# Weight sums by on-chip accumulating transfers, and the DVE order at the start of the feed-forward layer

## The chip, the cores and the metric

The kernel runs on one core of one Trainium2 chip. The metric is device time in microseconds of one launch. The kernel before the change took 1691.21 us (median of three runs, 1689.07 to 1691.75).

## The reference

Two layers work on `x` of 512 tokens by 1024 channels, all in float32. What matters here is the second half of the mixer and the feed-forward part:

```
for l in range(DEPTH):                       # DEPTH = 2
    h = rmsnorm(x, norm1_g[l])
    x = x + gated_parallel_mixer(h, ...)     # ends in: merged @ w_out, w_out 1024 x 1024
    h = rmsnorm(x, norm2_g[l])
    x = x + conv_ffn(h, w_up[l], conv_w[l], conv_b[l], w_down[l])
return rmsnorm(x, final_g)

def conv_ffn(h, w_up, conv_w, conv_b, w_down):
    u = h @ w_up                             # 1024 x 5632
    u = depthwise_conv_width_3(u, conv_w) + conv_b
    a, g = split(u, 2, axis=-1)
    return (gelu(g) * a) @ w_down
```

## The kernel before

**Layout and precision.** Everything is held transposed: channels on the 128 partitions, the 512 tokens along the free dimension. A float32 product is made of three matmuls. Each operand is split into a rounded high part and a low part that holds the rest, and `mm3` (lines 230 to 232) issues high by high, high by low and low by high. In the names of the trace `whi` and `wlo` are the two parts of a weight tile, `hh` and `hl` those of the normed activations, `mo` those of the merged mixer output.

**How a weight gets to TensorE.** `load` (line 135) or `load_sum` (line 165) brings it from HBM to an SBUF tile `raw`, of which there are three. `split` then makes the high part with a copy on ScalarE (line 216) and the low part with a subtraction on VectorE (line 217). The tiles `whi` and `wlo` have three buffers each. `weights` (line 202) is called at each product and calls `fetch`, which loads and splits for products up to two ahead of the one about to run. The loads are issued in program order on the SP queue, so a load that waits for a buffer holds up those behind it.

**The order of instructions.** TensorE and SP run in program order (`manual_schedule`). For the other engines a planner orders the instructions at build time, by priorities and a simulated timeline; each engine then runs its list strictly in that order. In `run` (line 416) some items of the list of work put VectorE under `manual_schedule` as well: `out`, `("two", 0)`, and the sums of `w_out` and of the second part of `w_down`. Such a region fixes the order of VectorE's instructions within one item. How the instructions of different items interleave stays with the planner.

**Sums of weights.** `w_out` is applied first by ordinary products (`do_out`, two of eight column blocks), then by three units `("sum", 2, m)` with m = 2, 4, 6 (`do_sum`, matmuls on lines 1047 to 1049). A unit covers two column blocks of 128 and uses a scheme of Strassen's kind: from the four quarter blocks V11, V12, V21, V22 of the weights it takes seven products, in the order V11, S1, V12, S2, S4, V22, S3, where S1 = V21 + V22, S2 = S1 + V11, S4 = S2 + V12 and S3 = V21 + V11. Each product multiplies four weight tiles of 128 by 128 with 256 columns, three matmuls each, so twelve matmuls. Two of the sums, S1 and S3, are not made by an engine for these units but by transfers. In `load_sum` the rows of V21 are loaded twice, once into a tile `raw` (this becomes S3) and once into a tile `ynl` (this becomes S1). Then GpSimd issues two accumulating transfers (line 172), which add the rows of V22 from HBM to `ynl`, and those of V11 from HBM to `raw`. Each is 256 KB, in pieces of 512 bytes. V11 and V22 also lie in tiles `ynh` of their own. The loads of a unit's first product are issued seven products ahead. There are six units in the kernel, three in each layer.

**Start of the feed-forward layer.** `do_up` without an argument runs the first four column blocks of `w_up` as a group: four PSUM banks, each product in two halves, eight weight tiles of 128 by 512. The tokens' norm is not applied to `h`; it is applied after the product, by a row `rb` that is spread over the partitions. `norm_sums` and `norm_spread` make it after the first half of the group: a reduction on VectorE, three small instructions on GpSimd, a small transfer and a broadcast on GpSimd (line 276). `conv` takes a product from PSUM: VectorE multiplies it by `rb` (`u`, line 223), ScalarE applies the middle tap and the bias (`c`, line 993), VectorE adds the outer taps (lines 994 and 995). For the gate half ScalarE then applies the gelu (line 999), VectorE multiplies (`prod`), and `operands` forms and splits the operands of the later `w_down` sums (`ft`, `tt`). Every further column block is an item `("up", f)` of its own: one product of 24 matmuls of 512 columns, then its `conv`. In the group the four convs are called after the second half of their product.

## Time and profile before

| what | value |
|---|---|
| median of three runs | 1691.21 us |
| the profiled execution | 1688.92 us |
| its span, first to last instruction | 1687.1 us |
| TensorE matmul busy | 1666.2 us, 99% of the span |
| TensorE weight load busy | 1416.9 us, 84% |
| VectorE busy | 1315.8 us, 78% |
| ScalarE busy | 915.3 us, 54% |
| GpSimd busy | 68.3 us, 4% |
| read from HBM | 156.61 MB |

Times in the trace count from the start of the span. The engines are PE (TensorE), PEld (its weight load), DVE (VectorE), ACT (ScalarE), POOL (GpSimd), and SP; a q behind the name is the engine's sequencer, which issues transfers. A row of the timeline gives start, duration, engine, line, operation, what is written and read, and in brackets how long the engine was idle before it and what released it. A matmul's duration is the time through the pipeline: in steady work a matmul of 512 columns shown as 0.39 us starts every 0.227 us, and one of 256 columns shown as 0.28 us every 0.12 us. So a PE that is shown 99% busy can still be waiting or running slowly, and one has to look at the distance between starts.

In layer 0 the `w_out` units run from about 447 to 484 us, the group of `w_up` from 484.6 to 506.8 us. In layer 1 the same happens about 835 us later.

### The profile page before, as it was taken

The page shows a single profiled execution, that of the slowest core. Times are in us where ns is not written, and L with a number is a line of the kernel's source. Part 1 is how long each engine was busy: PE and PEld are TensorE (multiplying, and loading weights), DVE is VectorE, ACT ScalarE, POOL GpSimd, SP SyncE. Part 2 cuts the span into 40 slices and gives each one's busy share as a digit, 9 for nine tenths or more (in the row PEclk, how much of TensorE's full clock was granted, in tenths as well). Part 3 has the DMA queues.
Part 4 walks back from the last instruction along what each step waited for, and adds up shares of the span by engine and source line. Part 5 has one row for each costly group of instructions (what it writes and reads, how often), then busy time and mean ns, then how long its engine had stood idle before and what let it go on. Part 6 is the DMA issues. An engine that isn't in the chain of part 4 may idle for free.

```text
span 1687.1 us, 24783 instructions
## 1 busy us (share of the span) xinstructions
PE 1666.2 (99%) x9379; PEld 1416.9 (84%) x9379; DVE 1315.8 (78%) x2267; ACT 915.3 (54%) x1617; POOL 68.3 (4%) x119
## 2 busy tenths in 40 slices
PE   9999999999999999999999999999999999999998
PEld 7888888888887889888987888888888788898888
DVE  7677866787769888787977687667887698987886
ACT  7664445775445444454567544467744454434454
POOL 1110000000110000000011100000001000000000
PEclk9999999999999999999999999999999999999999
DMA  6233323222643333333233333332236333324322
GB/s 183 70 98 89 90 77 89 79 69 76 136 108 103 97 103 95 103 100 97 77 105 82 89 84 94 82 88 67 66 91 138 106 104 100 96 84 121 100 82 82
DMA packets 299304, 160.35 MB, mean 95 GB/s; under 512 B 9552, under 2 KB 295264, under 8 KB 299184
## 3 DMA queue, kind: packets, MB, share of 16 engines
q1 hardware_dynamic: 290304, 150.45, 31.6%
q0 software_dynamic: 8592, 7.98, 2.4%
q8 instruction: 74, 1.21, 0.3%
q14 instruction: 46, 0.38, 0.1%
q10 hardware_dynamic: 288, 0.33, 0.1%
HBM read 156.61 MB, written 2.10 MB: 94 GB/s over the span
## 4 chain that ended last, share of the span: by engine, by line
PE 65%; DVE 1%; issue 1%; DMA 1%; ACT 0%; POOLq 0%; POOL 0%; SPq 0%; ACTq 0%
PE ps_d L232 10%; PE ps_d L231 10%; PE ps_d L230 10%; PE ps_ring L230 6%; PE ps_ring L231 6%; PE ps_ring L232 6%; PE ps_d L1049 4%; PE ps_d L1048 4%; PE ps_d L1047 4%; DMA ynl<-in_w_out_dram 1%; PE ps_ring L311 1%; PE ps_g L230 1%; PE ps_g L232 1%; PE ps_g L231 1%; PE ps_ring L298 1%
## 5 line engine op out<-in xcount | busy, mean ns | idle before, releaser
L216 ACT CAST whi<-raw 128x1024 fp32r<-128x1024 f32 (+4 forms) x344 | 291.2, 847 | 402.1 <-PE ps_ring L231 140.0
L217 DVE TENSOR_TENSOR wlo<-raw,whi 128x1024 fp32r<-128x1024 f32 (+4 forms) x342 | 331.6, 970 | 40.9 <-ACT whi L216 39.5
L232 PE MATMUL ps_d<-hh,wlo 128*128 128x512 f32 x685 | 268.2, 391 | 5.7 <-DVE wlo L217 5.7
L231 PE MATMUL ps_d<-hl,whi 128*128 128x512 f32 x685 | 267.7, 391 | 0.0
L230 PE MATMUL ps_d<-hh,whi 128*128 128x512 f32 x685 | 267.5, 391 | 0.0
L230 PE MATMUL ps_ring<-hh,whi 128*128 128x512 f32 x600 | 235.3, 392 | 0.8 <-DVE nm L909 0.3
L232 PE MATMUL ps_ring<-hh,wlo 128*128 128x512 f32 x600 | 233.7, 390 | 0.0
L231 PE MATMUL ps_ring<-hl,whi 128*128 128x512 f32 x600 | 233.6, 389 | 0.0
L232 PEld LDWEIGHTS ps_d<-hh,wlo 128*128 128x128 f32 x685 | 129.4, 189 | 33.4 <-DVE wlo L217 6.6
L230 PEld LDWEIGHTS ps_d<-hh,whi 128*128 128x128 f32 x685 | 129.5, 189 | 26.8
L231 PEld LDWEIGHTS ps_d<-hl,whi 128*128 128x128 f32 x685 | 129.2, 189 | 27.1
L1049 PE MATMUL ps_d<-ft,wlo 128*128 128x256 f32 x511 | 144.6, 283 | 0.0
L1048 PE MATMUL ps_d<-ft,whi 128*128 128x256 f32 x511 | 144.6, 283 | 0.0
L1047 PE MATMUL ps_d<-ft,whi 128*128 128x256 f32 x511 | 144.6, 283 | 0.0
L230 PEld LDWEIGHTS ps_ring<-hh,whi 128*128 128x128 f32 x600 | 112.6, 188 | 25.1 <-DVE pt L751 0.9
L232 PEld LDWEIGHTS ps_ring<-hh,wlo 128*128 128x128 f32 x600 | 112.7, 188 | 23.6
L231 PEld LDWEIGHTS ps_ring<-hl,whi 128*128 128x128 f32 x600 | 112.7, 188 | 23.1
L1048 PEld LDWEIGHTS ps_d<-ft,whi 128*128 128x128 f32 x511 | 98.1, 192 | 0.2
L1047 PEld LDWEIGHTS ps_d<-ft,whi 128*128 128x128 f32 x511 | 98.1, 192 | 0.2
L1049 PEld LDWEIGHTS ps_d<-ft,wlo 128*128 128x128 f32 x511 | 98.1, 192 | 0.0
L223 DVE TENSOR_TENSOR u<-ps_d,rb 128x512 f32<-128x512 f32 x80 | 54.9, 686 | 38.1 <-PE ps_d L232 37.8
L223 DVE TENSOR_TENSOR gz<-ps_ring,rb 128x512 f32<-128x512 f32 x44 | 30.4, 690 | 68.7 <-PE ps_ring L232 68.7
(365 smaller groups left out, 3364.3 us busy)
## 6 DMA issues: line engine op xcount, KB each, us to landing
raw<-in_w_in_dram SPq DMA_DIRECT2D x86, 512.0 KB, 4.0
raw<-in_w_up_dram SPq DMA_DIRECT2D x80, 512.0 KB, 3.8
raw<-in_w_down_dram SPq DMA_DIRECT2D x18, 384.0 KB, 3.7
own<-in_w_down_dram SPq DMA_DIRECT2D x16, 384.0 KB, 4.7
raw<-in_w_in_dram SPq DMA_DIRECT2D x17, 256.0 KB, 3.4
raw<-in_w_br_mla_dram SPq DMA_DIRECT2D x16, 256.0 KB, 2.7
raw<-in_w_br_na_dram SPq DMA_DIRECT2D x16, 256.0 KB, 2.7
raw<-in_w_br_gqa_dram SPq DMA_DIRECT2D x16, 256.0 KB, 2.7
```

What stands on the lines that cost most here:

```text
L216: nc.scalar.copy(hi, src)
L217: nc.vector.tensor_sub(lo, src, r32(hi))
L223: self.nc.vector.tensor_tensor(out, a, b, ALU.mult)
L230: mm(ps, sh, mh, start=first and k == 0, stop=False)
L231: mm(ps, sh, ml, start=False, stop=False)
L232: mm(ps, sl, mh, start=False, stop=last and k == n - 1)
L298: self.nc.tensor.transpose(out[2 * u + i][:, c * 64:c * 64 + 64], block[q], self.idf[q, q])
L311: self.nc.tensor.matmul(out, st[a], mv[b], start=first and t == 0, stop=last and t == 2)
L1047: mm(ps, wh, hi, start=fresh and i == 0, stop=False, skip_group_check=True)
L1048: mm(ps, wh, lo, start=False, stop=False, skip_group_check=True)
L1049: mm(ps, wl, hi, start=False, stop=i == n - 1, skip_group_check=True)
```

## The change

Two things are changed.

**Sums.** For the units of `w_out` the loads are issued in another order: V22 first, then the rows of V21 into `ynl`, then V11, then V21 into `raw`. Before it was V11, V21, V22, and then the rows of V21 again. The two accumulating transfers no longer read HBM: they read the tiles that hold V22 and V11 in SBUF, with 2 KB in one piece for each partition. The tile names change with the order (the two `ynl` tiles swap between units, and V22 and V11 swap their `ynh`).

**Order.** The items `up` and `("up", f)` for the first six feature blocks put VectorE under program order, item by item. In these items the convs are moved: the group no longer calls them; its four products go on a list `late`, and one is taken from it at the end of the group. Each later item first runs its product (in which `weights` splits the tiles of products to come), appends itself to the list, and takes two from it while there are two or more, else one. After three items the list is empty, and from then on an item runs its own conv as before.

```diff
     def load_sum(self, j, unit):
-        w = unit["np"] * P
-        for name in {0: ("V11", "V21", "V22"), 2: ("V12",)}.get(j, ()):
-            m, e = unit["m"] + int(name[1]) - 1, int(name[2]) - 1
-            if name in ("V11", "V22"):
+        w, loaded = unit["np"] * P, unit["part"] == 2
+        rows = lambda n: unit["w"][unit["r0"]:unit["r0"] + 2 * w, (unit["m"] + int(n[1]) - 1) * P:(unit["m"] + int(n[1])) * P] \
+            .rearrange("(i e p) c -> e p i c", e=2, p=P)[int(n[2]) - 1]
+        for name in {0: ("V22", "S1", "V11", "V21") if loaded else ("V11", "V21", "V22"), 2: ("V12",)}.get(j, ()):
+            if name == "S1":
+                t = self.mxt(f"ynl{self.owns // 2 % 2}")
+            elif name in ("V11", "V22"):
                 t = self.own(unit["part"], w)
             else:
                 t = self.wp.tile([P, 1024], F32, tag="raw", name="raw", bufs=RAWB)
             unit[name] = t[:, :w]
-            rows = unit["w"][unit["r0"]:unit["r0"] + 2 * w, m * P:(m + 1) * P].rearrange("(i e p) c -> e p i c", e=2, p=P)
-            self.nc.sync.dma_start(unit[name].rearrange("p (i c) -> p i c", c=P), rows[e])
-            unit["rows", name] = rows[e]
-        if j == 0 and unit["part"] == 2:
-            unit["S1"], unit["S3"] = self.mxt(f"ynl{self.owns // 2 % 2}"), unit["V21"]
-            view = lambda n: unit[n].rearrange("p (i c) -> p i c", c=P)
-            self.nc.sync.dma_start(view("S1"), unit["rows", "V21"])
-            for n, other in (("S1", "V22"), ("S3", "V11")):
-                self.nc.gpsimd.dma_start(view(n), unit["rows", other], accum_op=ALU.add)
+            self.nc.sync.dma_start(unit[name].rearrange("p (i c) -> p i c", c=P), rows("V21" if name == "S1" else name))
+        if j == 0 and loaded:
+            unit["S3"] = unit["V21"]
+            self.nc.gpsimd.dma_start(unit["S1"], unit["V22"], accum_op=ALU.add)
+            self.nc.gpsimd.dma_start(unit["S3"], unit["V11"], accum_op=ALU.add)
...
-                    elif item in ("out", ("two", 0)) or name == "sum" and args[0]:
+                    elif item in ("out", "up", ("two", 0)) or name == "up" and args[0] % NF < 6 or name == "sum" and args[0]:
                         with self.tc.manual_schedule(engines={mybir.EngineType.DVE}):
...
-            ups = [0, NF, 1, NF + 1]
-            conv = lambda *js: [self.conv(ups[j], self.gbank[j]) for j in js]
-            self.group(self.W["up"], self.h, {(0, 3): lambda: (self.norm_sums(), self.norm_spread()), (1, 0): lambda: conv(0), (1, 1): lambda: conv(1),
-                                              (1, 2): lambda: conv(2), (1, 3): lambda: conv(3)})
+            self.late = []
+            self.group(self.W["up"], self.h, {(0, 3): lambda: (self.norm_sums(), self.norm_spread())})
+            self.late = list(zip([0, NF, 1, NF + 1], self.gbank))
+            self.conv(*self.late.pop(0))
         else:
-            self.conv(fi, self.dense(self.spec(), self.h))
+            self.late.append((fi, self.dense(self.spec(), self.h)))
+            for _ in range(2 if len(self.late) > 1 else 1):
+                self.conv(*self.late.pop(0))
```

## The prediction

> **What bounds the kernel now.** I read the page first, then PE's waits, then the timeline of PE around the longest of them, and last windows around each place.

> ```profile
> span 1687.1 us, 24783 instructions
> PE 1666.2 (99%) x9379; PEld 1416.9 (84%) x9379; DVE 1315.8 (78%) x2267; ACT 915.3 (54%) x1617; POOL 68.3 (4%) x119
> ```

> TensorE is the bound: its busy time leaves 21 us of the span. No engine's total can be what the change works on; only places where PE stands still, or runs slowly, can. The list of PE's waits names them.

> ```profile
> PE ps_d L232 <- DVE wlo L217: 5.7, 2, 2.9
> PE ps_d L1047 <- ACT whi L216: 4.8, 3, 2.6
> ```

> (Total, number, longest.) The first is two stalls, one a layer, of a `w_up` product on a low part. The second is three stalls of the `w_out` sums on a high part. These are the two places of the change. The timeline of PE shows that a stall costs more than its gap:

> ```profile
> 448.83 0.28 PE L1049 MATMUL ps_d<-mo,wlo 128*128 128x256 f32 x1
> 451.73 0.39 PE L1047 MATMUL ps_d<-mo,whi 128*128 128x256 f32 x1 [2.62 <-ACT whi L216]
> 455.90 0.41 PE L1048 MATMUL ps_d<-mo,whi 128*128 128x256 f32 x1
> ...
> 507.07 0.39 PE L231 MATMUL ps_d<-hl,whi 128*128 128x512 f32 x1
> 510.34 0.50 PE L232 MATMUL ps_d<-hh,wlo 128*128 128x512 f32 x1 [2.88 <-DVE wlo L217]
> 512.16 0.63 PE L231 MATMUL ps_d<-hl,whi 128*128 128x512 f32 x1
> 512.58 0.63 PE L232 MATMUL ps_d<-hh,wlo 128*128 128x512 f32 x1
> ```

> After the stall at 507 the starts are 0.42 us apart (512.16 to 512.58). To price gap and slow stretch together I count matmuls in windows (columns: length, PE busy and count, PEld, DVE, ACT, POOL, granted clock, DMA share, GB/s).

> ```profile
> 457.00:459.00 2.00, 2.00 (x19) 2.00 (x18) 1.83 (x5) 1.05 (x2) 0.52 (x1) 1.00 0.39 103
> 518.00:529.00 11.00, 11.00 (x50) 9.13 (x49) 10.96 (x17) 6.62 (x10) 0.00 (x0) 1.00 0.45 131
> 448.90:456.00 7.10, 4.25 (x22) 3.85 (x22) 4.29 (x9) 4.54 (x8) 1.28 (x1) 0.78 0.34 42
> 473.90:480.00 6.10, 5.17 (x39) 4.51 (x38) 5.25 (x10) 3.58 (x6) 0.00 (x0) 1.00 0.02 5
> 1284.40:1290.00 5.60, 3.73 (x27) 3.12 (x26) 3.85 (x7) 4.24 (x8) 1.27 (x1) 1.00 0.41 50
> 1297.40:1302.00 4.60, 4.27 (x32) 3.81 (x32) 4.60 (x9) 2.77 (x5) 1.27 (x1) 1.00 0.68 118
> 1308.70:1313.00 4.30, 3.98 (x29) 3.53 (x29) 4.30 (x8) 2.55 (x5) 0.00 (x0) 1.00 0.01 2
> 507.10:515.10 8.00, 5.12 (x16) 3.77 (x15) 7.24 (x10) 4.36 (x5) 0.73 (x1) 0.79 0.27 78
> 1340.90:1349.00 8.10, 5.26 (x17) 3.97 (x16) 7.43 (x11) 4.55 (x5) 0.63 (x1) 0.79 0.30 86
> ```

> A count includes two matmuls that were still in the pipeline at the left edge. In the quiet rows that leaves 17 starts in 2.00 us, so 0.12 us for 256 columns, and 48 in 11.00, so 0.23 us for 512. A window's loss is its length less (count − 2) times that step:

> - sums, layer 0: 7.1 − 20 × 0.12 = 4.7, and 6.1 − 37 × 0.12 = 1.7;
> - sums, layer 1: 5.6 − 25 × 0.12 = 2.6; 4.6 − 30 × 0.12 = 1.0; 4.3 − 27 × 0.12 = 1.1;
> - feed-forward starts: 8.0 − 14 × 0.227 = 4.8, and 8.1 − 15 × 0.227 = 4.7.

> The sums lose 11.1 us, the feed-forward starts 9.5, together 20.6 us. That is the most that the change can be meant to win.

> **The sums, part by part.** Four loads on SP and two accumulating transfers on POOL a unit stay four and two. What changes is the order, the source and the piece size. Layer 0, first unit, before:

> ```profile
> 433.49 0.46 SPq L165 DMA_DIRECT2D ynh<-in_w_out_dram  x1
> 435.79 0.37 SPq L165 DMA_DIRECT2D raw<-in_w_out_dram  x1
> 436.76 0.50 SPq L170 DMA_DIRECT2D ynl<-in_w_out_dram  x1
> ...
> 439.63 1.39 POOL L172 DMA_DIRECT2D raw<-in_w_out_dram  x1 [238.54 <-DMA ynh<-in_w_out_dram]
> 445.13 1.29 POOL L172 DMA_DIRECT2D ynl<-in_w_out_dram  x1 [4.11 <-DMA raw<-in_w_out_dram]
> 451.29 1.28 POOL L172 DMA_DIRECT2D raw<-in_w_out_dram  x1 [4.87 <-issue]
> 456.24 1.27 POOL L172 DMA_DIRECT2D ynl<-in_w_out_dram  x1 [3.67 <-issue]
> ...
> 451.06 0.62 ACT L216 CAST whi<-ynl 128x512 fp32r<-128x512 f32 x1 [5.62 <-DMA ynl<-in_w_out_dram]
> 451.71 0.69 DVE L217 TENSOR_TENSOR wlo<-ynl,whi 128x512 fp32r<-128x512 f32 x1 [4.67 <-ACT whi L216]
> 462.23 0.62 ACT L216 CAST whi<-ynl 128x512 fp32r<-128x512 f32 x1 [0.77 <-DMA ynl<-in_w_out_dram]
> ```

> Two delays add up for S1. Its base load stands last on SP, behind a `raw` that waited for its buffer until 435.79. And the planner put S3's accumulation ahead of it; POOL's transfers go one at a time, 5.0 to 6.2 us apart (439.63, 445.13, 451.29, 456.24). So S1, the second product of seven, is summed after S3, the last one.

> After: V22 takes the place of V11 at 433.49 and S1's base follows 0.5 us later, with no `raw` ahead of it. It lands by about 438.4, with the time to landing of these rows:

> ```profile
> ynl<-in_w_out_dram SPq DMA_DIRECT2D x6, 256.0 KB, 4.4
> ynl<-in_w_out_dram POOLq DMA_DIRECT2D x6, 256.0 KB, 5.4
> rope<-in_rope_dram POOLq DMA_DIRECT2D x6, 256.0 KB, 3.2
> ```

> The accumulation of S1 is then ready first, and I expect POOL to issue it at 438.7. It must land by 447.8 to cost PE nothing: PE could start at 448.95, the cast takes 0.62 and the subtraction 0.69, and the low part is needed 0.24 after the start.

> The new price is that of accumulating from SBUF, which no row shows. Bounds: 3.2 us (a plain load of the same size on the same queue, `rope`) and 6.2 us (the longest step between two accumulations). I take 5.4: nearest is the same operation into the same tile from HBM. S1 lands at 444.1, 3.7 us early; at the ends, 441.9 or 444.9. The added waits (S1's transfer now also waits for V22's landing, S3's for V11's) come last in neither case, since V22 and V11 are issued ahead of their partners. Queued behind a waiting POOL is only the next accumulation.

> At 5.4 a transfer, one at a time, in the order S1, S3, S1, S3, S1, S3, the second unit's S1 lands at 438.7 + 3 × 5.4 = 454.9. Before, its cast at 462.23 caused no loss in PE; with the first stall gone PE is 4.7 earlier, so it is needed by 457.5: 2.6 early. The third unit's S1 lands at 438.7 + 5 × 5.4 = 465.7. PE stalled for it from 474.0 on, so with 1.2 for the split and PE 4.7 earlier it is needed by 468.1: 2.4 early. So all three stalls of a layer go, and the follow-on waits on low parts with them. I take 10.7 of the 11.1 us. If the cover were gone, each microsecond over 5.9 a transfer costs 5 us a layer (five transfers in series before the third S1).

> **The feed-forward start.** DVE, ACT and POOL in layer 0:

> ```profile
> 501.38 1.05 ACT L216 CAST whi<-raw 128x1024 fp32r<-128x1024 f32 x1 [2.10 <-PE ps_g L231]
> 508.59 0.81 ACT L993 ACTIVATE c<-u,x 128x512 f32<-128x512 f32 x1 [6.16 <-DVE u L223]
> ...
> 506.62 1.21 POOL L276 PARTITION_BROADCAST rb<-row  x1 [6.93 <-issue]
> ...
> 507.86 1.29 DVE L223 TENSOR_TENSOR u<-ps_g,rb 128x512 f32<-128x512 f32 x2 [7.86 <-POOL rb L276]
> 509.07 1.22 DVE L217 TENSOR_TENSOR wlo<-raw,whi 128x1024 fp32r<-128x1024 f32 x1
> 510.20 1.40 DVE L994 SCALAR_TENSOR_TENSOR c<-u,x,c 128x511 f32<-128x511 f32 x2
> ```

> The high part that PE needs was done at 502.43. The subtraction for its low part takes 1.22 us, and DVE was idle for 7.86. But the list of DVE had two multiplications by `rb` ahead of it, and `rb` came at 506.62 + 1.21 = 507.83. It is an order fault, with nothing missing. After, the region of the group holds the low parts of the next two products ahead of its one conv: the first at 502.5 to 503.7, PE needs it at 507.3; the second follows its high part, whose buffer comes free when PE is done with the group's seventh tile. The eighth takes 12 × 0.227 = 2.7 us and ends at 506.84 (one step before the start at 507.07), so that is 504.1; cast until 505.2, subtraction until 506.4. Both are done before `rb` arrives, so no conv starts later for it, and DVE has 2.4 us less to do after 507.86.

> What is late next? The product after these two needs its low part at 518; its region has it first, ahead of two convs. PSUM: eight banks, so a product may run up to seven ahead of its conv; it now runs about four ahead. I take 9.3 of the 9.5 us, and nothing for the moved convs, covered as follows. PE is 4.8 us earlier and DVE 2.4 us, so DVE's lag grows by 2.4. DVE was full in 518 to 529 (10.96 of 11.00, above), and then:

> ```profile
> 551.00:562.00 11.00, 11.00 (x50) 9.09 (x50) 8.39 (x13) 4.65 (x7) 0.00 (x0) 1.00 0.33 96
> ```

> It has 2.6 us free here, where it waits for PE. The lag is made up long before the `w_down` sums, near 630. If that cover were gone, the 2.4 us would come back.

> **The slow stretches.** Of the losses, 4.8 − 3.0, 4.7 − 3.0 and 4.7 − 3.2, about 5.0 us, are not gap but slow starts behind it (gap and first follow-on wait taken off). The rows have them behind gaps of 2.62 and 2.88 us, with a granted clock of 0.78 and 0.79 in those windows, and of 1.00 where the gap was shorter (1284), so I count them as part of the stall and let them go with it. [...]

> **The sum.** 10.7 + 9.3 = 20.0 us. The profiled execution took 1688.92 us around its span of 1687.1, so it should become 1668.9; it lies 2.3 under the median, and from the median the same step gives 1691.2 − 20 = 1671.2. I predict 1671.

> **Rivals.** (1) Only the feed-forward start gains: the planner still puts S3 first, or the accumulation from SBUF has a longer latency that gives back what the order won. For: POOL is not under program order. Against: V21's `raw` still waits for its buffer, so S3 is ready later. Time: 1691.2 − 9.3 = 1681.9. (2) Only the sums gain: ACT's list is still the planner's, and the high part of a later product could stand behind the convs' casts, with `rb` in front of them. For: ACT did nothing between 502.43 and 508.59, and then a conv's tap came first. Against: the second low part must precede the conv, so ACT cannot reverse it. Time: 1691.2 − 10.7 = 1680.5. (3) Slower: POOL's chain of accumulations becomes the bound of the sums. At T a transfer the third S1 lands at 438.7 + 5T and is needed by 468.1, so a layer stalls for 5T − 29.4, and two stalls add 1.5 us each of slow starts (4.7 − 3.2, as above). The time is 1671.2 + 2 × (5T − 26.4) once T is above 5.9. It is slower than before from T = 7.3 on; at T = 9 it is 1708. For: the transfer reads and writes SBUF, untried here. Against: 6.2 is the top of the rows, and the pieces are larger. (4) Nothing happens: the planner's own new order gives stalls of the same size elsewhere, so 1691. (5) The stalls go and the slow stretches stay, from a cause that is not the gap: 1671.2 + 5.0 = 1676. Against: the clock row of the shorter gap.

> **How the numbers follow.** Forecast 0.76, rival 1 0.07, rival 2 0.05, rival 5 0.02, rival 4 0.04, rival 3 0.06. A run of this kernel can tell about 0.2%, 3.4 us, from no change. Faster is 0.76 + 0.07 + 0.05 + 0.02 = 0.90, same 0.04, slower 0.06. The low end is the profiled execution less all of the 20.6, 1668.3, less 2 us for an order of the planner's that happens to be better: 1666. The high end takes in rivals 1, 2 and 5: 1682. That leaves out about 0.1 for rivals 3 and 4, and a little.

> **What the changed profile should show.** PE's waits on `whi` at line 1047 and on `wlo` at line 232 gone, with no window of a granted clock near 0.8 at either place. On POOL the `ynl` accumulation first, issued within 1 us of its base's landing, and a time to landing between 3.2 and 6.2. On DVE two low parts of 1024 columns between 502 and 507, ahead of the first `u`. PE busy time falls little, the span by 20. I am wrong if POOL's transfers follow one another at more than 5.9 us, if `raw` is still first on POOL, or if new PE waits appear before 560 (DVE behind) or at the start of the `w_down` sums.

## The result and the profile after

The kernel after takes 1667.14 us (median of four runs, 1666.46 to 1667.93). The kernel before took 1690.43 beside it (four runs, 1689.07 to 1691.75). The ratio is 0.9862, 95% interval 0.9845 to 0.988, a gain of 23.3 us. The profiled execution took 1666.98 us, 21.9 less than that of before. Of all the runs below, one of before and one of the kernel with the old load order took 2045 us at a mean granted clock of 0.75; medians and ranges leave these two out.

Line numbers shift a little between the kernels. In the kernel after, `split` is on lines 215 and 216, `mm3` on 229 to 231, and the matmuls of the sums are on 1048 to 1050.

The page of the kernel after: the span, the engines' busy times, the packets of GpSimd's queue, the bytes from HBM, and the shares of the chain that ended last.

```profile
span 1665.1 us, 24804 instructions
PE 1656.6 (99%) x9379; PEld 1411.7 (85%) x9379; DVE 1316.5 (79%) x2267; ACT 915.8 (55%) x1617; POOL 62.9 (4%) x119
q0 software_dynamic: 3984, 7.98, 2.0%
HBM read 153.47 MB, written 2.10 MB: 93 GB/s over the span
PE 97%; DVE 2%; ACT 1%; issue 0%; DMA 0%; ACTq 0%
```

In the page of before, GpSimd's queue reads:

```profile
q0 software_dynamic: 8592, 7.98, 2.4%
```

TensorE now carries 97% of the chain that ended last, so little is left to wait for. (The page of before has no chain to set beside it: its shares add up to 68%, since the chain is followed only part of the way back there.) HBM reads fell by 3.14 MB (156.61 before), which is twelve transfers of 256 KB. The waits of PE say the same; these are the longest that are left (total, number, longest):

```profile
PE idle L428 <- DVE cst L89: 1.0, 1, 1.0
PE ps_ring L229 <- DVE pt L750: 1.0, 6, 0.2
PE ps_ring L229 <- DVE nm L908: 0.6, 2, 0.3
```

Both waits of the prediction are gone and none has come in their place. GpSimd's and ScalarE's part of the first unit of layer 0, from the timeline after:

```profile
438.66 0.92 POOL L170 DMA_DIRECT2D ynl<-ynh  x1 [237.64 <-DMA ynl<-in_w_out_dram]
440.16 0.86 POOL L171 DMA_DIRECT2D raw<-ynh  x1 [0.57 <-DVE ynl L838]
446.07 0.62 ACT L215 CAST whi<-ynl 128x512 fp32r<-128x512 f32 x1 [0.74 <-PE ps_d L230]
```

S1's accumulation (`ynl`) goes first, at 438.66, and the second follows 1.5 us later, not after the landing of the first. By the trace's landing times the first took 5.70 us to 444.36. The cast of S1 came at 446.07 and waited for TensorE, not for the transfer.

VectorE at the start of the feed-forward part, and the broadcast that its first `u` waits for:

```profile
495.52 1.23 DVE L216 TENSOR_TENSOR wlo<-raw,whi 128x1024 fp32r<-128x1024 f32 x1 [2.46 <-ACT whi L215]
498.24 1.23 DVE L216 TENSOR_TENSOR wlo<-raw,whi 128x1024 fp32r<-128x1024 f32 x1 [1.49 <-ACT whi L215]
500.80 0.69 DVE L222 TENSOR_TENSOR u<-ps_g,rb 128x512 f32<-128x512 f32 x1 [1.33 <-POOL rb L275]
```

The two low parts fill what was VectorE's idle wait for `rb`, and `u` starts with `rb`'s arrival as it did before the change. The windows of the kernel after over the two places in layer 0 (columns as in the prediction):

```profile
448.00:456.00 8.00, 8.00 (x69) 8.00 (x68) 7.67 (x16) 5.56 (x11) 0.85 (x1) 1.00 0.55 121
499.90:507.90 8.00, 8.00 (x37) 6.63 (x36) 6.47 (x8) 5.18 (x6) 0.86 (x1) 1.00 0.46 135
```

By the prediction's count, (69 − 2) × 0.12 = 8.04 and (37 − 2) × 0.227 = 7.95 us: nothing is lost in either, at a granted clock of 1.00.

**A finer measure of the same loss.** From here on I add up, over a stretch, how far each matmul's start lies beyond the regular step behind the last one (0.226 us for 512 columns, 0.120 for 256). "Sums" is the stretch of the `w_out` units in both layers, "start" that of the feed-forward starts. In the profile before this gives 12.0 and 9.6 us, against the 11.1 and 9.5 counted from windows. The two stretches of after, without a stall, give 0.2 each.

| profile of | sums | start | profiled time |
|---|---|---|---|
| before | 12.0 | 9.6 | 1688.92 |
| before, once more | 13.5 | 8.0 | 1688.79 |
| after | 0.2 | 0.2 | 1666.98 |
| sums' part alone | 0.3 | 9.6 | 1676.27 |
| the same, once more | 0.3 | 8.0 | 1674.39 |
| order's part alone | 17.1 | 0.3 | 1684.74 |
| before, larger scratch | 6.0 | 6.4 | 1679.61 |
| after, sums from HBM | 1.3 | 0.2 | 1668.85 |
| after, old load order | 0.3 | 0.2 | 1667.81 |
| after, no fixed order | 0.3 | 7.8 | 1675.10 |
| the same, once more | 0.5 | 9.7 | 1677.69 |
| after, early convs | 0.2 | 32.1 | 1699.41 |
| after, fixed order in the group only | 0.3 | 0.2 | 1667.72 |

In each row the two columns, less the 0.4 of after, give the distance of its time from that of after to within 1 us. So the differences of these kernels lie in the two places.

### The profile page after: what moved, and what is told of

It reads as the page before. It is cut to its first block, busy times and chain, and to the rows that moved or that the text cites. A ratio compares the mean times of both kernels' runs of the same rounds, so it can differ in the third digit from the quotient of the medians.

```text
span 1665.1 us, 24804 instructions
## 1 busy us (share of the span) xinstructions
PE 1656.6 (99%) x9379; PEld 1411.7 (85%) x9379; DVE 1316.5 (79%) x2267; ACT 915.8 (55%) x1617; POOL 62.9 (4%) x119
## 3 DMA queue, kind: packets, MB, share of 16 engines
q0 software_dynamic: 3984, 7.98, 2.0%
q8 instruction: 74, 1.21, 0.3%
## 4 chain that ended last, share of the span: by engine, by line
PE 97%; DVE 2%; ACT 1%; issue 0%; DMA 0%; ACTq 0%
PE ps_ring L229 13%; PE ps_ring L230 12%; PE ps_ring L231 12%; PE ps_d L230 11%; PE ps_d L229 11%; PE ps_d L231 11%; PE ps_d L1050 5%; PE ps_d L1049 5%; PE ps_d L1048 5%; PE ps_ring L310 2%; PE ps_g L231 2%; PE ps_g L229 2%; PE ps_g L230 2%; PE ps_ring L297 1%; PE ps_ring L778 1%; PE ps_g L330 1%
## 5 line engine op out<-in xcount | busy, mean ns | idle before, releaser
L216 DVE TENSOR_TENSOR wlo<-raw,whi 128x1024 fp32r<-128x1024 f32 (+4 forms) x342 | 331.8, 970 | 52.7 <-ACT whi L215 51.0
L231 PE MATMUL ps_d<-hh,wlo 128*128 128x512 f32 x685 | 266.5, 389 | 0.0
L231 PE MATMUL ps_ring<-hh,wlo 128*128 128x512 f32 x600 | 233.7, 390 | 0.0
L231 PEld LDWEIGHTS ps_d<-hh,wlo 128*128 128x128 f32 x685 | 128.6, 188 | 26.7
L1049 PE MATMUL ps_d<-ft,whi 128*128 128x256 f32 x511 | 144.6, 283 | 0.0
L1048 PE MATMUL ps_d<-ft,whi 128*128 128x256 f32 x511 | 144.6, 283 | 0.0
L231 PEld LDWEIGHTS ps_ring<-hh,wlo 128*128 128x128 f32 x600 | 112.6, 188 | 23.6
L230 PEld LDWEIGHTS ps_ring<-hl,whi 128*128 128x128 f32 x600 | 112.7, 188 | 23.1
L1048 PEld LDWEIGHTS ps_d<-ft,whi 128*128 128x128 f32 x511 | 98.1, 192 | 0.2
L1049 PEld LDWEIGHTS ps_d<-ft,whi 128*128 128x128 f32 x511 | 98.1, 192 | 0.2
## 6 DMA issues: line engine op xcount, KB each, us to landing
raw<-in_w_in_dram SPq DMA_DIRECT2D x17, 256.0 KB, 3.4
raw<-in_w_br_mla_dram SPq DMA_DIRECT2D x16, 256.0 KB, 2.7
raw<-in_w_br_na_dram SPq DMA_DIRECT2D x16, 256.0 KB, 2.7
raw<-in_w_br_gqa_dram SPq DMA_DIRECT2D x16, 256.0 KB, 2.7
```

The source lines that it names most:

```text
L216: nc.vector.tensor_sub(lo, src, r32(hi))
L230: mm(ps, sh, ml, start=False, stop=False)
L231: mm(ps, sl, mh, start=False, stop=last and k == n - 1)
L1048: mm(ps, wh, hi, start=fresh and i == 0, stop=False, skip_group_check=True)
L1049: mm(ps, wh, lo, start=False, stop=False, skip_group_check=True)
```

## The experiments

My theory was the prediction's: two independent order faults, each with its stall, whose gains add. The rivals were that only one part gains, that the gain of the sums comes from the on-chip source and not from the order (or the reverse), and that the slow stretches have another cause than the gaps. The first four kernels ran beside a before of 1691.73 us (seven runs, 1689.47 to 1694.2). A ratio is the kernel's time over that of the before beside it, with its 95% interval.

**The sums' part alone.** The kernel before with the new `load_sum`:

```diff
-        for name in {0: ("V11", "V21", "V22"), 2: ("V12",)}.get(j, ()):
+        for name in {0: ("V22", "S1", "V11", "V21") if loaded else ("V11", "V21", "V22"), 2: ("V12",)}.get(j, ()):
...
+            self.nc.gpsimd.dma_start(unit["S1"], unit["V22"], accum_op=ALU.add)
+            self.nc.gpsimd.dma_start(unit["S3"], unit["V11"], accum_op=ALU.add)
```

> The kernel before with the new load order and the on-chip accumulations alone. Theory (the two edits act at separate stalls and add up): the three stalls of the sums in each layer go, worth 11.1 us in the windows of before, and the stall at the start of the feed-forward layer stays with its 9.5 us: about 1679.5 us, and PE still waits for a low part twice, 2.9 us each. Rival (the edits help each other, since the planner orders both anew): clearly off the sum, below 1676 or above 1683.

Measured: 1676.28 us (1675.42 to 1676.29), ratio 0.9905 (0.9891 to 0.992). The longest wait of PE:

```profile
PE ps_d L231 <- DVE wlo L216: 5.6, 2, 2.8
```

The waits of the sums are gone, that of the start stands as it was. By the medians the gain is 15.5 us, 13.5 to 18.4 by the interval. That is more than the 11.1 I counted: the time is 3.2 us below the 1679.5 that I expected, and close to the 1676 below which I would have taken the rival. By the table the two places are still independent here: the loss of the sums goes from 12.0 to 0.3, that of the start stays at 9.6.

**The order's part alone.** The kernel before with the other two hunks of the change:

```diff
-                    elif item in ("out", ("two", 0)) or name == "sum" and args[0]:
+                    elif item in ("out", "up", ("two", 0)) or name == "up" and args[0] % NF < 6 or name == "sum" and args[0]:
...
+            self.late = list(zip([0, NF, 1, NF + 1], self.gbank))
+            self.conv(*self.late.pop(0))
```

> The kernel before with the new order of VectorE and the late convs alone. Theory (separate stalls): the feed-forward stall goes, the stalls of the sums stay: 1690.4 - 9.5 = about 1681 us, with PE waiting for the high part in the sums three times, up to 2.6 us. Rival (edits help each other): off the sum by more than 3 us.

Measured: 1684.16 us (1683.36 to 1684.74), ratio 0.9953 (0.9938 to 0.9968), a gain of 7.6 (5.4 to 10.5 by the interval). The wait of the start is gone. The longest wait left (line 1049 is the first matmul of the sums in this kernel):

```profile
PE ps_d L1049 <- ACT whi L216: 8.7, 4, 3.2
```

That is the wait of the sums, and longer than in the profile before (4.8, 3, 2.6). GpSimd's rows in layer 1 show one reason:

```profile
1270.35 1.37 POOL L172 DMA_DIRECT2D raw<-in_w_out_dram  x1 [238.56 <-DMA ynh<-in_w_out_dram]
1277.36 1.30 POOL L172 DMA_DIRECT2D ynl<-in_w_out_dram  x1 [5.65 <-DMA ynh<-in_w_out_dram]
1282.11 1.27 POOL L172 DMA_DIRECT2D raw<-in_w_out_dram  x1 [3.44 <-issue]
```

S1's accumulation came 7.0 us behind S3's, where it was 5.4 in layer 1 of the profile before. Whether the edit or chance made it so is open. The time is 3.2 us above my 1681, past the 3 us that I had named as the rival's sign. But I had subtracted from the 1690.4 of earlier runs; from the before beside it, 1691.73, the miss is 1.9, inside the interval. The two parts gain 15.5 + 7.6 = 23.1 us, and the whole change 23.3: within intervals of about 2.5 us to either side, no interaction shows.

**Before, with twice the scratch space.** In the profile before, the second accumulation was issued 0.3 us after the first had landed (444.81 to 445.13), and so the next (450.96 to 451.29). One parameter of the kernel, a scratch space of 2048 bytes (`dynamic_dma_scratch_size`), could be what holds it. That GpSimd's transfers need this space was my guess, and this run tests it:

```diff
-    nc = _bacc.Bacc("TRN2", target_bir_lowering=False, num_devices=1, dynamic_dma_scratch_size=2048)
+    nc = _bacc.Bacc("TRN2", target_bir_lowering=False, num_devices=1, dynamic_dma_scratch_size=4096)
```

> The kernel before, unchanged but for the space that is set aside for the descriptors of transfers issued by GpSimd, 4096 bytes for 2048; every engine's order is that of before. Theory (the accumulations follow one another only because the space holds one transfer of 512-byte pieces): the accumulation of S1 is issued right behind that of S3, at about 441.3 instead of 445.1, lands by 447, and the sums' stalls shrink by 8 to 11 us: 1680 to 1683 us. Rival (the wait is a semaphore or a dependency between the two): issue at 445.1 as before and 1690 us.

Measured: 1680.32 us (1678.55 to 1683.43), ratio 0.9933 (0.9916 to 0.9949). From its timeline:

```profile
439.46 1.39 POOL L172 DMA_DIRECT2D raw<-in_w_out_dram  x1 [238.60 <-DVE ynl L837]
441.61 1.29 POOL L172 DMA_DIRECT2D ynl<-in_w_out_dram  x1 [0.76 <-DMA ynl<-in_w_out_dram]
450.31 0.62 ACT L216 CAST whi<-ynl 128x512 fp32r<-128x512 f32 x1 [4.96 <-DMA ynl<-in_w_out_dram]
450.98 0.39 PE L1047 MATMUL ps_d<-mo,whi 128*128 128x256 f32 x1 [1.96 <-ACT whi L216]
```

Two accumulations are now under way at once: 2.15 us apart, not 5.5. So the space was what made them serial; what it holds, no run shows. S1 still landed late, at 450.21 where I had expected 447: it took 8.60 us, beside S3's transfer and loads of the SP queue. The first stall of each layer stays, those of the later units go: the sums lose 6.0 us, so about half of their stall goes (6.0 of 12.0), not the 8 to 11 us that I expected. That the time still fell in my 1680 to 1683 is partly luck: in this profile neither feed-forward start has a slow stretch behind its gap (6.4 us in place of 9.6).

**After, with the sums from HBM.** The new order of loads and accumulations, but the old source and its pieces of 512 bytes:

```diff
-            self.nc.gpsimd.dma_start(unit["S1"], unit["V22"], accum_op=ALU.add)
-            self.nc.gpsimd.dma_start(unit["S3"], unit["V11"], accum_op=ALU.add)
+            for n, other in (("S1", "V22"), ("S3", "V11")):
+                self.nc.gpsimd.dma_start(unit[n].rearrange("p (i c) -> p i c", c=P), rows(other), accum_op=ALU.add)
```

> The changed kernel with its new load order, but with the accumulations reading V22 and V11 from HBM in 512-byte pieces as before; the order of every engine is that of the changed kernel. Theory (the order made the gain, S1 ahead of S3 and its base ahead of the buffer wait): transfers 5.0 to 6.2 us apart still bring every S1 in time, no stall in the sums, 1667 to 1669 us. Rival (the source made it): the second or third S1 of a unit comes late, stalls of 1 us and more return, 1671 to 1678 us.

Measured: 1669.15 us (1668.16 to 1670.15), ratio 0.9865 (0.9849 to 0.9882), at the upper end of what I expected. Its rows on GpSimd, and the first cast:

```profile
438.44 1.39 POOL L171 DMA_DIRECT2D ynl<-in_w_out_dram  x1 [237.29 <-DMA ynl<-in_w_out_dram]
445.53 1.29 POOL L171 DMA_DIRECT2D raw<-in_w_out_dram  x1 [5.70 <-DMA ynh<-in_w_out_dram]
446.24 0.62 ACT L215 CAST whi<-ynl 128x512 fp32r<-128x512 f32 x1 [0.74 <-PE ps_d L230]
```

The accumulations are serial again, S1's took 6.77 us, and its cast still waited for PE alone. The order by itself takes away all but about 1 us of the sums' stalls.

The next four ran beside a before of 1692.08 us (seven runs, 1690.56 to 1695.65).

**After, with the old load order.** The on-chip source, but S3's accumulation first:

```diff
-        for name in {0: ("V22", "S1", "V11", "V21") if loaded else ("V11", "V21", "V22"), 2: ("V12",)}.get(j, ()):
+        for name in {0: ("V11", "V21", "V22", "S1") if loaded else ("V11", "V21", "V22"), 2: ("V12",)}.get(j, ()):
```

> The kernel after, with the accumulations taken from the on-chip tile, but the loads and so the accumulations in the order before: S3's goes first on GpSimd's queue, S1's base is the fourth load. My theory: with 2 KB pieces two transfers are under way together, so S1's is issued about 2.5 us later than after (near 441.2) and lands 5 to 7 us later (446 to 448.2), at or just past its need: 0 to 1 us of stall in each first unit, 1667 to 1670. Rival: the order alone makes the gain (the kernel with HBM as source and the new order kept it), then the sums' stalls are back, 2 us and more with the slow clock behind them in each layer, 1673 to 1678.

Measured: 1667.98 us (three runs, 1667.81 to 1668.19), ratio 0.9852 (0.9835 to 0.987). From its timeline:

```profile
440.28 0.92 POOL L171 DMA_DIRECT2D raw<-ynh  x1 [238.50 <-DMA ynh<-in_w_out_dram]
442.19 0.86 POOL L170 DMA_DIRECT2D ynl<-ynh  x1 [0.99 <-PE ps_d L231]
447.80 0.62 ACT L215 CAST whi<-ynl 128x512 fp32r<-128x512 f32 x1 [1.65 <-DMA ynl<-ynh]
```

S1 landed 5.45 us after its issue, at 447.64, and the cast waited for it. TensorE did not: the sums lose no more than after. So the source by itself is enough too, but with less to spare than the whole change: there S1 had landed at 444.36 and the cast waited for TensorE. Each half of the sums' part removes nearly the whole stall; with neither it is 17.1 us (order's part alone).

**After, without the fixed order on VectorE.**

```diff
-                    elif item in ("out", "up", ("two", 0)) or name == "up" and args[0] % NF < 6 or name == "sum" and args[0]:
+                    elif item in ("out", ("two", 0)) or name == "sum" and args[0]:
```

> The kernel after, with the first convolutions called after the group as there, but without the hand-written order on VectorE: the planner places those steps by cost and due time, and its order puts both first u (which wait for the broadcast rb) ahead of the two 128x1024 low parts of the third ahead tile, as before. My theory: it is the place of these low parts on VectorE that sets the start of the feed-forward stage, so TensorE waits about 3 us again in each layer and runs at the slow clock after it: +9.5 us, about 1676.5 (1675 to 1678), with 'wlo' as releaser of the wait. Rival: calling the convolutions later is enough, because the broadcast is early enough; then within 1 us of 1667.

Measured: 1674.85 us (1673.23 to 1676.18), ratio 0.9892 (0.9874 to 0.991). That is just under the 1675 to 1678 that I expected, at a start loss of 7.8 us in its profile (9.7 in the repeat below). The wait on `wlo` is back, and from the timeline of PE:

```profile
503.66 0.50 PE L231 MATMUL ps_d<-hh,wlo 128*128 128x512 f32 x1 [2.72 <-DVE wlo L216]
```

Calling the convs later does nothing alone: this kernel and the sums' part alone (1676.28) are 1.4 us apart, and this kernel's own runs spread by 2.95. The rival, that the late call suffices, is out.

**After, with the convs called in the group.**

```diff
-            self.late = []
-            self.group(self.W["up"], self.h, {(0, 3): lambda: (self.norm_sums(), self.norm_spread())})
-            self.late = list(zip([0, NF, 1, NF + 1], self.gbank))
-            self.conv(*self.late.pop(0))
+            ups = [0, NF, 1, NF + 1]
+            conv = lambda *js: [self.conv(ups[j], self.gbank[j]) for j in js]
+            self.group(self.W["up"], self.h, {(0, 3): lambda: (self.norm_sums(), self.norm_spread()), (1, 0): lambda: conv(0), (1, 1): lambda: conv(1),
+                                              (1, 2): lambda: conv(2), (1, 3): lambda: conv(3)})
...
-            self.late.append((fi, self.dense(self.spec(), self.h)))
-            for _ in range(2 if len(self.late) > 1 else 1):
-                self.conv(*self.late.pop(0))
+            self.conv(fi, self.dense(self.spec(), self.h))
```

> The kernel after, with the hand-written order on VectorE, but the four first convolutions called within the group as before. VectorE's program order then holds the first u (which waits for rb, ready at 500.8 in the profile after) ahead of the group's last 128x512 low part, and then two convolutions ahead of the first 128x1024 one. My theory: TensorE waits for these low parts from about 496 to beyond 503 and again behind the next convolution, some 8 to 12 us in each layer with the slow clock after it: slower than before, 1685 to 1695. Rival: order and call place do the same thing, each by itself, and the time stays at 1667; or the order alone does nothing, and it is 1676.5.

Measured: 1699.34 us (1699.26 to 1699.64), ratio 1.004 (1.0026 to 1.0054): slower than before by 0.4%. Rows of its VectorE in layer 0, and the two longest waits of PE:

```profile
490.14 0.68 DVE L216 TENSOR_TENSOR wlo<-raw,whi 128x512 fp32r<-128x512 f32 x1
500.52 0.69 DVE L222 TENSOR_TENSOR u<-ps_g,rb 128x512 f32<-128x512 f32 x1 [9.70 <-POOL rb L275]
...
503.54 0.69 DVE L216 TENSOR_TENSOR wlo<-raw,whi 128x512 fp32r<-128x512 f32 x1
```

```profile
PE ps_g L231 <- DVE wlo L216: 12.5, 2, 6.3
PE ps_d L231 <- DVE wlo L216: 10.1, 2, 5.2
```

The next low part of the group stands behind a `u` that waits 9.7 us for `rb`, and PE waits for it. The direction and the place were as expected, the size was not: 16 us in each layer, where I had 8 to 12.

**Before, once more.** No edit; a second profile.

> The kernel before, once more, for its profile. My theory: the landing times of GpSimd's accumulations from HBM vary from execution to execution (5.0 to 6.9 us seen), and with them the stalls of the sums, so the excess of TensorE in the two windows of the sums differs from the 11.8 us of the profile before (11 to 18), while the excess at the start of the feed-forward stage stays at 9.4 (within 0.3). Rival: the stalls are the same in each execution and the spread of 5 us comes from elsewhere; then both stay within 0.5.

Measured: 1688.79 us. Its waits:

```profile
PE ps_d L1047 <- ACT whi L216: 6.6, 4, 2.6
PE ps_d L232 <- DVE wlo L217: 5.6, 2, 2.8
```

The stalls of the sums do differ, four and 6.6 us here against three and 4.8. The loss at the start was expected to stay within 0.3 and did not: 8.0 us instead of 9.6, at gaps of nearly the same length. That part of my theory fell, and the next runs look into it.

The last three ran beside a before of 1690.45 us (seven runs, 1686.58 to 1696.31).

**After, with the fixed order in the group only.**

```diff
-                    elif item in ("out", "up", ("two", 0)) or name == "up" and args[0] % NF < 6 or name == "sum" and args[0]:
+                    elif item in ("out", "up", ("two", 0)) or name == "sum" and args[0]:
```

> The kernel after, with the hand-written order kept for the group's own item and dropped for the feed-forward tiles behind it. My theory: what counts is that the two 128x1024 low parts of the third ahead tile stand ahead of the first u on VectorE; this kernel's VectorE order has them there too, so there is no wait of TensorE at the start of the feed-forward stage: 1666.5 to 1668.5. Rival: the later tiles need the hand-written order as well, since the planner puts their low parts behind pairs of u and c steps; then a wait of 1 us or more on 'wlo' appears between 503 and 520 in each layer: 1670 to 1676.

Measured: 1667.38 us (1666.66 to 1667.82), ratio 0.986 (0.983 to 0.989), the same as after. The fixed order of the six tiles behind the group is not needed. That of the group's own item is, which puts the two low parts ahead of the first `u`: without it the wait is back (1674.85).

**Two kernels once more, for the clock.** After without the fixed order, and the sums' part alone; no new edit.

> The kernel with late convolutions and no hand-written order, once more, for its profile. Theory: whether the slow clock follows a gap of 2.9 us is a matter of the moment at which the gap falls, not of its length or place: the two gaps again measure 2.9 (within 0.1), and each costs either 3.0 (clock stays at 1.00) or 4.7 us (clock at 0.50 for some 3.5 us), not always in the same layer as in the first profile (layer 0 without, layer 1 with). Rival: it is fixed by what runs around the gap; then layer 0 again shows none and layer 1 again shows it.

> The kernel before with the sums' part alone, once more, for its profile. Theory: as there, its two gaps measure 2.9 to 3.0 us and each costs 3.0 or 4.7 us by the moment at which it falls; no stall of the sums in either layer. Rival: both gaps cost 4.7 us again, as in its first profile.

Measured: 1677.69 and 1674.39 us. Two windows show the question: sums' part alone and then after without the fixed order, in their first profiles, just behind the gap in layer 0. The third column from the right is the granted clock.

```profile
504.00:506.00 2.00, 2.00 (x6) 1.58 (x5) 2.00 (x3) 0.84 (x1) 0.00 (x0) 0.50 0.79 232
```

```profile
504.00:506.00 2.00, 2.00 (x10) 1.65 (x9) 2.00 (x4) 1.32 (x2) 0.00 (x0) 1.00 0.50 135
```

The gaps were 2.91 and 2.88 us, the clock behind them 0.50 and 1.00. (A gap is here, as in the finer measure, how far a start lies beyond the regular step. The timeline's bracket counts from the end of the matmul before, and has 2.72 for the second.) In the repeat of the second kernel layer 0, which had no slow stretch, now has one (4.6 us instead of 3.1); in the repeat of the first kernel layer 1 lost its own (3.2 instead of 4.8 us). So neither the kernel nor the place in the program fixes it. Seven profiles have this stall in both layers, 14 gaps of 2.84 to 3.14 us: nine cost 4.6 to 5.0 us and five 3.0 to 3.2. One of my numbers was off: the second gap of the first repeat measured 3.14, more than 0.1 from 2.9.

The clock records of the traces say what goes with it. The three slow stretches of the profile before, in windows that just hold them:

```profile
452.90:456.31 3.41, 3.41 (x18) 3.41 (x17) 3.41 (x8) 2.70 (x5) 0.07 (x1) 0.50 0.62 77
510.92:514.33 3.41, 3.41 (x10) 2.64 (x9) 3.41 (x6) 1.26 (x3) 0.00 (x0) 0.50 0.53 154
1343.78:1347.19 3.41, 3.15 (x7) 2.48 (x8) 3.41 (x6) 1.91 (x3) 0.00 (x0) 0.50 0.53 154
```

Behind each of the nine gaps the stretch at 0.50 lasts 3.41 us, and within a profile all changes of the clock lie whole multiples of 3.41 us apart: the starts above are 17 and 244 such steps from one to the next. On this grid the five gaps without a slow stretch begin 1.8 to 2.3 us behind a step. The nine with one begin 2.4 us or more behind a step, or up to 0.7 us behind the next. So among these 14 the point of the grid at which a gap begins separates the two cases without an exception.

## Why the prediction was right

**The bound and the places.** Right. Removing the two stalls took the loss in the two places from 21.6 to 0.4 us, and the kernels with one part each show that the parts add up, as far as their intervals can tell. Rivals 1 and 2 (one part alone) and 4 (nothing) are out by the waits after. One slip: "all three stalls of a layer" fits layer 1; the windows of layer 0 show two (from 448.9 and from 473.9).

**The sum.** 20.0 us was forecast, 21.9 came between the two profiled executions and 23.3 between the medians. So the time came 3.9 below the 1671, and 1.1 above the low end of the range, which stood for an order that happens to be better and not for what happened. By the finer measure the two places gave 21.6 − 0.4 = 21.2 us, 1.2 more than the terms; the other 0.7 of the 21.9 lie outside them. The 1.4 from there to the medians is the profile before being 1.5 below its median (and that of after 0.2 below its own). I took the step from the median, but with stalls read from one execution, and these vary: 12.0 and 13.5 us for the sums in two profiles of before. The kernels with one part put the terms elsewhere: 15.5 us for the sums' part against 10.7, which its interval (13.5 to 18.4) leaves out, and 7.6 for the order's part against 9.3, which its interval holds. So the term of the sums was too small, and that the total came nearer than this term is partly luck.

**S1's transfer.** The issue was forecast at 438.7 and came at 438.66; the landing at 444.1 came at 444.36. The price of 5.4 us was near for this one (5.70), which runs beside the loads. It is not a price of the operation: seven of the twelve accumulations after took 3.25 to 3.36 us, the other five 4.6 to 7.2, among them the first two of each layer, which run beside loads. The need at 447.8 is borne out from both sides, roughly: with the old load order S1 landed at 447.64 and PE lost nothing, in a profile where the sums begin 0.7 us later than in that of before; with the larger scratch it landed at 450.21, 2.4 past that point, and PE stood for 2.0.

**The step that failed: one transfer at a time.** "POOL's transfers go one at a time" was read rightly from before and carried over wrongly. After, the second is issued 1.5 us behind the first. In layer 0 the S1 of the second and third units landed at 450.46 and 461.75, where the serial chain of the prediction had 454.9 and 465.7. The larger scratch shows that it was space, not the queue, that made them serial: 5.5 us between issues with 2048 bytes, 2.15 with 4096. With pieces of 2 KB from SBUF, 2048 bytes were enough for two at a time. That such a transfer needs less of the space is my estimate, which no run shows by itself; it goes by the packets: GpSimd's queue has 3984 packets in place of 8592, and 4608 over twelve accumulations is 384 fewer each. So rival 3, built on a serial chain, could not have come in the form that I gave it. Even where the chain was serial, with the sums from HBM in the new order, the sums lost about 1 us.

**The feed-forward start.** Right in mechanism and size. Both low parts were done by 498.24 + 1.23 = 499.47, ahead of `rb` (the `u` at 500.80), no conv started later for them, and no PE wait appears before 560. Rival 2's reason, that ScalarE's list could reverse it, did not come true. What I did not see is that the order and the late call hold only together: the late call without the order gains nothing at the start, and the order without the late call is 32.2 us worse than with it, and slower than before. That was the slower case nearest to this change, and it was not among my rivals.

**The slow stretches.** They went with the gaps, so rival 5 is out. But I took them as part of each stall, "The rows have them behind gaps of 2.62 and 2.88 us", and at about such lengths they came at 9 of 14. The length of a gap does not separate the two cases: one of 2.91 us had the clock at 0.50 behind it (sums' part alone, layer 0), and one of 3.02 us had it at 1.00 (the repeat of that kernel, layer 1). In the traces the clock changes on a grid of 3.41 us, and the gaps fall on it differently from run to run. That the point of the grid makes the difference rests on the split of the 14 gaps; no run set it on purpose.

**The spread.** The runs of before range from 1686.6 to 1696.3 us, those of after from 1666.5 to 1667.9. Two things vary in before and cost nothing after: when the serial accumulations land, and the clock behind a gap (about 1.6 us at each).

## What to carry to other kernels

Where an engine waits for a value that arrives late, look at what stands behind the wait in its list: moving independent work ahead of it cost nothing here (0.2 us of loss left at the start, of 9.6), but fixing the order while the waiting call stays early can be worse than leaving it to the planner (1699.34 us here, beside 1692.08). A stall of some microseconds that depends on a transfer's landing should be read from more than one profile before it is priced: the sums lost 12.0 and 13.5 us in two profiles of before. And of two remedies for the same deadline, test each alone: here either the order or the source of the transfers was enough (1669.15 and 1667.98 us), and the pair bought slack.
